# A hybrid decoder layer on one core: the loads of late operands move to ScalarE's DMA queue, and plain output copies enter ScalarE's written order

## The chip, the cores and the metric

The kernel runs on one core of a Trainium2 chip. Its engines work side by side and meet through semaphores: TensorE (PE; its weight loads are PEld), VectorE (DVE), ScalarE (ACT), GpSimd (POOL) and SyncE (SP). Transfers are started by an instruction in the order of one engine (here SP, POOL and, rarely, ACT), and are carried by 16 DMA engines. The metric is the device time of one execution in microseconds (us): the median of the runs shown, 2655.42 us before the change.

## The reference

One layer over 512 tokens of width 2048, in float32. It adds three branches to the residual x, one after the other:

```python
[u | v_sgu | q | k | v_att | g_a | g_b] = rmsnorm(x, attn_norm_g) @ w_in
y_a = u * (tril(W_s) v_norm + b)              # gMLP, chunks of 128
y_b = stick_breaking_attention(q, k, v_att)
x = x + (sigmoid(g_a) * (y_a @ w_up_a) + sigmoid(g_b) * (y_b @ w_up_b)) @ w_o
gate, up = split(rmsnorm(x, ffn_norm_g) @ w_ffn_in)        # hidden width 5632
x = x + (silu(gate) * up) @ w_ffn_out
x = x + sigmoid(rmsnorm(x, ple_norm_g) @ w_ple_gate) * (p @ w_ple)
```

## The kernel before

**Arithmetic.** Activations stand transposed (features on 128 partitions, 512 tokens along a row). Each float32 product is made of three fp32r products of a high and a low part. So every weight block and every operand block is split in two: ACT copies the high part (L369 for weights `whi`, L289 for operands `parts`), and DVE subtracts it to give the low part (L366 `wlo`, L290 `parts`). L385 and L540 are DVE sums of blocks that the cheaper scheme below needs.

**Pairs.** The unit of work is a pair: two 128-wide output tiles, accumulated over units of 256 features. A unit of kind "P" is plain (PE lines L299, L300, L301, three products for each piece). A unit of kind "S" uses a Strassen-like scheme with seven or so products of sums of blocks (PE line L716), whose results are put together from PSUM banks by ACT copies (L739, L772) and DVE adds (L742, L775). A pair may have both kinds: its first part runs plain while the operands' sums are not there yet. `Pair.out()` (L808) finishes a pair. For an all-plain pair it copies two banks with ACT (L814). For a mixed pair `rest()` (L817) adds the two plain banks to the result with DVE (L821).

**Operands.** A form (a set of operand parts of one unit) is built from a block that `load` (L529) fetches from DRAM: `y_form` from the stored y, `spilled_form` (L1392) from the stored mix, x1, hid and x2. A "late" form first makes its plain parts, and later fetches the blocks of sums that were stored beside hid (`second_blocks`, L1379: one transfer of 768 columns and one of 256). `wholes` is the name of every loaded block in the profile.

**Stages**, in us of the profiled execution: the embedding's first pair and start (0 to 92), the w_in pairs with the spatial gating and attention (to 762), the merge with w_up (to 1007), w_o (to 1160), FFN-in (44 pairs, to 2031), FFN-out in three passes over the hidden width, each with its own operands (2031 to 2192, to 2353, to 2490), and the gate (to 2651). At each change of stage PE goes from one set of operands to the next, and that set is loaded and split while PE runs the last pair of the stage behind it.

**Order.** Instructions are traced in the order of the code; a scheduler with a cost model then fixes the order on each engine. `in_turn` binds an ACT or DVE instruction to the one traced before it on that engine, so that such instructions keep the written order. Splits, sums and the copies of the products are in turn; L814 and L821 are not, and the scheduler places them. DMAs go in the order of their issuing engine: SP carries nearly all weights, spills and loads, POOL the accumulating loads (L373), and ACT only the two halves of pT (the layer's input embedding p) at the start. Each DMA that SP or ACT starts is given one of eight completion semaphores in rotation; one that takes a semaphore over waits in its engine's order until that semaphore's last transfer has landed.

Of the kernel before, what the change touches and what calls it, by code (L numbers as in the profile page):

```python
# [14 lines left out]
AF = mybir.ActivationFunctionType  # L15
# [5 lines left out]
T = 512  # L21
# [49 lines left out]
def hybrid_layer(  # L71
# [18 lines left out]
    nc = tc.nc  # L90
# [25 lines left out]
    class Arena:  # L116
# [5 lines left out]
        def take(self, n, how="low"):  # L122


            spots = []
            for start, size in self.holes:
                end = start + size
                if how == "place":
                    start = -(-start // (2 * PLACE)) * 2 * PLACE
                if end - start >= n:  # L130
                    if how == "high":
                        spots.append((-end, end - n))
                    elif how != "old":
                        spots.append((start, start))
                    else:
                        spots.extend((self.given[a // P : -(-(a + n) // P)].max(), a)
                                     for a in {*range(start, end - n + 1, 256), end - n})
            at = min(spots)[1]
            start, size = next(h for h in self.holes if h[0] <= at < h[0] + h[1])
            self.holes.remove((start, size))  # L140
            self.holes.extend(
                h for h in ((start, at - start), (at + n, start + size - at - n)) if h[1])
            return Block(self, at, n)
# [34 lines left out]
    def wide():  # L178
        return tmp.tile([P, 1024], F32, tag="out", name=nm("out"))
# [20 lines left out]
    def mark(instruction):  # L200
        newest[instruction.ins.engine] = instruction.ins.name
# [116 lines left out]
    def in_turn(*instructions):  # L318

        for i in instructions:  # L320
            e = i.ins.engine
            if e in chain:
                tc.add_manual_dep(
                    i.ins, chain[e],
                    mybir.DependencyInfo(mybir.DependencyClass.NoSync,
                                         mybir.DependencyReason.DATA),
                    reason="in its place among the weights")
            chain[e] = i.ins.name
            mark(i)
# [122 lines left out]
    def plain_weights(src):  # L452
        return Weights(src.rearrange("p (b c) -> p b c", b=4), 1, "P")
# [72 lines left out]
    def cut(x):  # L526
        return x.rearrange("p (b c) -> p b c", c=256)

    def load(src, n=1024, how="old"):  # L529
        b = take(n, how)  # L530
        nc.sync.dma_start(out=b.f(0, 1024), in_=src)
        return b

    def gained(dst, src, gi, k):
        return [nc.scalar.activation(dst[:, i * T : (i + 1) * T], src[:, i * T : (i + 1) * T],
                                     AF.Copy, scale=gcol[:, gi + 2 * k + i : gi + 2 * k + i + 1])
                for i in range(2)]
# [97 lines left out]
    def plain_form(src, ready=always, gain=None, raw=1024, how="low", far=False):  # L635
        def steps(form):
            hi, lo = form.blocks = parts.take(1024, how), parts.take(1024, how)
            w = form.raw()
            if gain:
                gained(hi.own(), w.f(), *gain)  # L640
                gi, k = gain
                for i in range(2):
                    a, b = i * T, (i + 1) * T
                    nc.vector.scalar_tensor_tensor(
                        out=lo.own(a, b), in0=w.f(a, b),
                        scalar=gcol[:, gi + 2 * k + i : gi + 2 * k + i + 1], in1=hi.f(a, b),
                        op0=ALU.mult, op1=ALU.subtract)
            else:
                split_into(hi.own(), lo.own(), w.f())
            give(w)  # L650
            return tuple([x.own(0, T), x.own(T)] for x in form.blocks)
            yield

        return Form("P", steps, [(parts, 1024, how)] * 2 + [(wholes, raw, "low")] * bool(raw),
                    ready, src, far)

    class Pair:
# [150 lines left out]
        def out(self, o=None):  # L808
            if self.n["S"]:
                assert o is None  # L810
                return self.rest(self.o)
            o = wide() if o is None else o
            for i, ps in enumerate(self.ends()):
                nc.scalar.activation(o[:, i * T : (i + 1) * T], ps, AF.Copy)  # L814
            return o

        def rest(self, o):  # L817
# [67 lines left out]
    ple_spill = {}  # L885
    ps_p = []

    def ple_raw(queue):
        raw = take(1024, "old")
        for k in (0, T):  # L890
            queue.dma_start(out=raw.f(k, k + T), in_=pT[:, k : k + T])
        return raw

    def ple_operands(raw=None):
        first = raw is not None
        raw = raw or ple_raw(nc.sync)
        ps_p.extend(parts.take(1024, "high") for _ in range(2))
        for k in (0, T):
            ops = split_into(*(x.own(k, k + T) for x in ps_p), raw.f(k, k + T))
            if first:  # L900
                in_turn(*ops)
        give(raw)
# [30 lines left out]
        x_raw.append(take(1024, "old"))  # L933
        nc.sync.dma_start(out=x_raw[-1].f(), in_=xT[len(x_raw) - 1])

    p_raw = ple_raw(nc.scalar)
    nc.scalar.preload_act_table_set("natural_log_exp_and_others")
    ones = consts.tile([P, P], F32, name="ones")
    nc.vector.memset(ones, 1.0)
    warm = small_bank()  # L940
    for _ in range(7):
        nc.tensor.matmul(warm[:, :P], ones, ones, start=True, stop=True)
    w_early = [plain_weights(w_ple[i]) for i in range(3)]
    load_x()
    gcol = consts.tile([P, ng], F32, name="gcol")
    nc.sync.dma_start(out=gcol, in_=gains)
# [99 lines left out]
    y_a, y_b = [None] * 4, [None] * 4  # L1046
    y_spill = [tc.dram_tile([P, 1024], F32, name=nm("y")) for _ in range(4)]
# [283 lines left out]
            plan(w_gate[j], now(GATE, GATE_UNTIL, j))  # L1331

    def y_form(c, i):
        return plain_form((lambda: y_a[i]) if c == "a" else lambda: load(y_spill[i]),
                          lambda: len(y_done) == 8, raw=0 if c == "a" else 1024,
                          far=c == "b")

# [2 lines left out]
    for n, ((w, i), pr) in enumerate(zip(order, made())):  # L1340
# [7 lines left out]
        o = pr.out(block(w, i) if n < 3 else None)  # L1348
# [17 lines left out]
        else:  # L1366
            d = tc.dram_tile([P, 1024], F32, name=nm("gsp"))
# [7 lines left out]
    spill = {(n, j): tc.dram_tile([P, 1024], F32, name=nm(n)) for n in ("mix", "x1", "x2")  # L1375
             for j in range(KU)}
    there, sum_spill = set(), {}

    def second_blocks(d):  # L1379
        blocks = take(768, "old"), take(256, "old")  # L1380
        nc.sync.dma_start(out=blocks[0].f(), in_=d[:, 256:1024])
        nc.sync.dma_start(out=blocks[1].f(), in_=d[:, 0:256])
        return blocks

    def summed_form(kind, n, j):
# [5 lines left out]

    def spilled_form(kind, n, j, gain=None, **how):  # L1392
        return (late_form if kind == "S" else plain_form)(
            lambda size=1024: load(spill[n, j], size), lambda: (n, j) in there, gain, far=True,
            **how)

    def store(n, j, block):
# [79 lines left out]
    for m in range(KH):  # L1477
        if m == KH - 1:
            build(hs[0])
        o = pair(fs, last=m == KH - 1, j=m, until=FFN_UNTIL, doubled=7).out()  # L1480
# [11 lines left out]
    for c, units in enumerate(hs):  # L1492
# [3 lines left out]
        for j in range(KU):  # L1496
# [6 lines left out]
            o = pr.out()  # L1503
            if not end:
                after(2, lambda o=o, j=j: nc.gpsimd.dma_start(
                    out=spill["x1", j], in_=o, accum_op=ALU.add))
# [8 lines left out]
    for j in range(KU):  # L1515
# [36 lines left out]
        else:  # L1552
            o = pair(gs, j=j, until=GATE_UNTIL, doubled=5).out()
# [92 lines left out]
```

## Time and profile before

| | before |
|---|---|
| median of 3 runs | 2655.42 us (2654.60 to 2657.17) |
| profiled execution | 2658.68 us, span 2657.0 us |
| granted TensorE clock, mean | 0.998 |
| PE busy | 2634.6 us, 99% |
| DVE busy | 2265.8 us, 85% |
| ACT busy | 1408.5 us, 53% |
| POOL busy | 455.7 us, 17% |
| DMA moved | 574.32 MB, mean 216 GB/s |

An instruction's row gives its start, its duration, engine, line and tiles, and in brackets the idle time ahead of it with what ended it. Matmuls are pipelined, so the distance between starts, not the duration, is what one costs. A window's row gives its length, the busy time of PE, PEld, DVE, ACT and POOL with the count of instructions, the granted clock, the DMA share and GB/s.

### The profile page before, as it was taken

Reading aid. Unit: us, or ns where it says so; the run is one execution under the profiler, and the core shown is the slowest. Engines: PE = TensorE matmul, PEld = TensorE weight load, DVE = VectorE, ACT = ScalarE, POOL = GpSimd, SP = SyncE. Lnnn points to the kernel's source line nnn. Section 1 sums busy time; section 2 is a strip of 40 time slices with the busy share of each in tenths; the row PEclk is TensorE's granted clock in tenths of the full one; section 3 lists DMA queues with packets and bytes.
Section 4 is the critical chain, followed back from the end, with each engine's and each line's share of the span. In section 5 each row is a group of like instructions: output and inputs, shape, how many; then the busy total and the mean of one; then the engine's idle time right before and its main releaser. Section 6 shows DMA issues by size and latency. Waiting matters only on the chain.

```text
span 2657.0 us, 42520 instructions
## 1 busy us (share of the span) xinstructions
PE 2634.6 (99%) x15197; PEld 2302.2 (87%) x15197; DVE 2265.8 (85%) x3886; ACT 1408.5 (53%) x2263; POOL 455.7 (17%) x565
## 2 busy tenths in 40 slices
PE   9999999999999999999999999999999999999999
PEld 7888888888998888888888888888888888889888
DVE  8687878787887558999999999999999888879798
ACT  7757565655554335465444444444446445455543
POOL 0222323232210001101111111111111211211010
PEclk9999999999999999999999999999999999999999
DMA  6776777777775668987988888888888999988794
GB/s 207 184 195 171 195 171 195 170 191 185 176 190 191 222 222 263 260 245 206 248 223 225 217 219 213 214 220 218 208 224 244 255 227 290 214 249 272 223 269 136
DMA packets 301829, 574.32 MB, mean 216 GB/s; under 512 B 27441, under 2 KB 143921, under 8 KB 301617
## 3 DMA queue, kind: packets, MB, share of 16 engines
q1 hardware_dynamic: 238688, 452.05, 51.8%
q0 software_dynamic: 62640, 119.04, 27.8%
q8 instruction: 119, 1.95, 0.3%
q14 instruction: 94, 0.76, 0.1%
q10 hardware_dynamic: 288, 0.52, 0.1%
HBM read 509.64 MB, written 61.87 MB: 215 GB/s over the span
## 4 chain that ended last, share of the span: by engine, by line
PE 90%; DVE 5%; DMA 2%; ACT 1%; issue 1%; POOL 0%; DVEq 0%; SPq 0%; ACTq 0%; POOLq 0%
PE ps L716 55%; PE ps L301 8%; PE ps L300 8%; PE ps L299 8%; PE small L716 6%; DVE wlo L366 2%; PE small L1196 1%; PE small L1144 1%; DVE out L775 1%; PE small L1070 1%; DVE parts L290 1%; DMA wholes<-hid 1%; DVE wholes L385 1%; DMA wholes<-w_gate 0%; DVE wholes L540 0%
## 5 line engine op out<-in xcount | busy, mean ns | idle before, releaser
L716 PE MATMUL ps<-parts,whi 128*128 128x512 f32 x4486 | 1503.9, 398 | 5.6 <-ACT out L814 3.2
L369 ACT ACTIVATE whi<-wholes 128x512 fp32r<-128x512 f32 (+2 forms) x940 | 873.1, 946 | 742.6 <-DVE wholes L385 300.3
L366 DVE TENSOR_TENSOR wlo<-wholes,whi 128x512 fp32r<-128x512 f32 (+2 forms) x940 | 988.5, 1087 | 91.1 <-ACT whi L369 90.7
L716 PEld LDWEIGHTS ps<-parts,wlo 128*128 128x128 f32 x4486 | 843.1, 188 | 190.9 <-issue 1.9
L716 PE MATMUL ps<-parts,wlo 128*128 128x256 f32 x4486 | 887.9, 279 | 0.6 <-DVE wlo L366 0.6
L716 PEld LDWEIGHTS ps<-parts,whi 128*128 128x128 f32 x4486 | 724.0, 189 | 15.9 <-ACT out L814 3.8
L301 PE MATMUL ps<-parts,wlo 128*128 128x256 f32 (+1 forms) x1546 | 512.8, 333 | 1.1 <-DVE wlo L366 1.1
L300 PE MATMUL ps<-parts,whi 128*128 128x256 f32 (+1 forms) x1546 | 512.8, 332 | 0.7 <-DVE parts L290 0.7
L299 PE MATMUL ps<-parts,whi 128*128 128x256 f32 (+1 forms) x1537 | 509.0, 332 | 3.0 <-ACT parts L289 1.6
L385 DVE TENSOR_TENSOR wholes<-wholes 128x256 f32<-128x256 f32 x832 | 353.0, 424 | 15.5 <-DMA wholes<-w_ffn_out 0.8
L775 DVE TENSOR_TENSOR out<-out,ps 128x256 f32<-128x256 f32 x537 | 222.2, 417 | 131.8 <-ACT out L772 131.3
L300 PEld LDWEIGHTS ps<-parts,whi 128*128 128x128 f32 x1546 | 292.1, 189 | 35.1 <-DVE parts L290 1.7
L299 PEld LDWEIGHTS ps<-parts,whi 128*128 128x128 f32 x1537 | 290.7, 189 | 31.7 <-ACT parts L289 2.3
L301 PEld LDWEIGHTS ps<-parts,wlo 128*128 128x128 f32 x1546 | 292.4, 189 | 28.6 <-DVE wlo L366 1.5
L373 POOL DMA_DIRECT2D wholes<-w_ffn_in x169 | 147.3, 871 | 705.2 <-DVE wholes L385 216.7
L373 POOL DMA_DIRECT2D wholes<-w_in x132 | 117.5, 893 | 543.4 <-DMA wholes<-w_in 165.7
L716 PE MATMUL small<-parts,whi 128*128 128x512 f32 x496 | 197.0, 397 | 0.0
L772 ACT ACTIVATE out<-ps 128x256 f32<-128x256 f32 x285 | 105.8, 383 | 61.1 <-PE ps L716 52.0
L290 DVE TENSOR_TENSOR parts<-wholes,parts 128x1024 fp32r<-128x1024 f32 (+3 forms) x147 | 124.9, 867 | 12.2 <-ACT parts L289 12.1
L289 ACT ACTIVATE parts<-wholes 128x768 fp32r<-128x768 f32 (+3 forms) x147 | 107.9, 764 | 49.1 <-DVE wholes L540 19.2
L373 POOL DMA_DIRECT2D wholes<-w_ffn_out x70 | 61.0, 871 | 348.1 <-DVE out L775 68.6
L1458 ACT ACTIVATE out<-out 128x512 f32<-128x512 f32 x44 | 27.8, 632 | 174.0 <-DVE out L1265 174.0
(136 smaller groups left out, 1843.7 us busy)
## 6 DMA issues: line engine op xcount, KB each, us to landing
wholes<-w_ffn_in SPq DMA_DIRECT2D x169, 384.0 KB, 5.6
wholes<-w_in SPq DMA_DIRECT2D x132, 384.0 KB, 4.9
wholes<-w_ffn_in SPq DMA_DIRECT2D x169, 256.0 KB, 4.6
wholes<-w_ffn_in POOLq DMA_DIRECT2D x169, 256.0 KB, 5.4
wholes<-w_in SPq DMA_DIRECT2D x132, 256.0 KB, 3.9
wholes<-w_in POOLq DMA_DIRECT2D x132, 256.0 KB, 4.9
wholes<-w_ffn_out SPq DMA_DIRECT2D x70, 384.0 KB, 6.4
wholes<-x SPq DMA_DIRECT2D x46, 512.0 KB, 5.9
```

The lines of the kernel that those rows point to most:

```text
L289: return (nc.scalar.activation(hi, src, AF.Copy), nc.vector.tensor_tensor(out=lo, in0=src, in1=hi.bitcast(F32), op=ALU.subtract))
L290: nc.vector.tensor_tensor(out=lo, in0=src, in1=hi.bitcast(F32), op=ALU.subtract))
L299: nc.tensor.matmul(ps, sh, mh, start=start, stop=False)
L300: nc.tensor.matmul(ps, sh, ml, start=False, stop=False)
L301: return nc.tensor.matmul(ps, sl, mh, start=False, stop=stop)
L366: in_turn(nc.vector.tensor_tensor(out=self.lo[:, blocks], in0=r, in1=h.bitcast(F32), op=ALU.subtract))
L369: in_turn(nc.scalar.activation(h, r, AF.Copy))
L373: nc.gpsimd.dma_start(out=raw[:, 3:5], in_=self.src[:, 1:3], accum_op=ALU.add)
L385: in_turn(nc.vector.tensor_tensor(out=o, in0=x, in1=y, op=ALU.add))
L716: m = nc.tensor.matmul(out, l, r, start=first and k == 0, stop=last and k == 1)
L772: in_turn(nc.scalar.activation(out, x, AF.Copy, scale=scale))
L775: in_turn(nc.vector.tensor_tensor(out=out, in0=x, in1=y, op=op))
```

## The change

`load` gets a queue. The blocks of y, mix, x1, hid and x2 for operand forms, and both transfers of `second_blocks`, are started by ACT in place of SP: 112 transfers (4 of y, 16 of mix, 16 of x1, 22 first blocks of hid, 40 for second blocks of hid, 14 of x2). The residual and gate loads stay with SP. The L814 copies, 16 of them, enter ACT's written order. At the start, the second half of pT goes to SP, behind the first weights of the embedding.

```diff
-    def load(src, n=1024, how="old"):
+    def load(src, n=1024, how="old", queue=nc.sync):
         b = take(n, how)
-        nc.sync.dma_start(out=b.f(0, 1024), in_=src)
+        queue.dma_start(out=b.f(0, 1024), in_=src)
...
             for i, ps in enumerate(self.ends()):
-                nc.scalar.activation(o[:, i * T : (i + 1) * T], ps, AF.Copy)
+                in_turn(nc.scalar.activation(o[:, i * T : (i + 1) * T], ps, AF.Copy))
...
-    def ple_raw(queue):
+    def ple_raw(*queues):
         raw = take(1024, "old")
-        for k in (0, T):
-            queue.dma_start(out=raw.f(k, k + T), in_=pT[:, k : k + T])
+        for k, q in zip((0, T), queues):
+            q.dma_start(out=raw.f(k, k + T), in_=pT[:, k : k + T])
...
-    p_raw = ple_raw(nc.scalar)
+    w_early = [plain_weights(w_ple[0])]
+    p_raw = ple_raw(nc.scalar, nc.sync)
...
-    w_early = [plain_weights(w_ple[i]) for i in range(3)]
+    w_early.extend(plain_weights(w_ple[i]) for i in range(1, 3))
...
     def y_form(c, i):
-        return plain_form((lambda: y_a[i]) if c == "a" else lambda: load(y_spill[i]),
+        return plain_form((lambda: y_a[i]) if c == "a" else lambda: load(y_spill[i], queue=nc.scalar),
...
-        nc.sync.dma_start(out=blocks[0].f(), in_=d[:, 256:1024])
-        nc.sync.dma_start(out=blocks[1].f(), in_=d[:, 0:256])
+        nc.scalar.dma_start(out=blocks[0].f(), in_=d[:, 256:1024])
+        nc.scalar.dma_start(out=blocks[1].f(), in_=d[:, 0:256])
...
-            lambda size=1024: load(spill[n, j], size), lambda: (n, j) in there, gain, far=True,
+            lambda size=1024: load(spill[n, j], size, queue=nc.scalar), lambda: (n, j) in there, gain, far=True,
```

The lines behind about L940 count one more after the change (L1460 is L1461 and so on). The order of instructions shifts on every engine, also where no edited line stands. Three places follow; `wlo` and `whi` are parts of weights, `parts` those of operands, `ps` and `small` PSUM banks, `out` a pair's result.

DVE, early in FFN-in, just behind its first pair; before:

```order
L366 TENSOR_TENSOR wlo1_78<-wholes_74,whi1_77 128x512
L1460 TENSOR_TENSOR out_1275_11137<-out_1275_11137 128x512
L290 TENSOR_TENSOR parts_73<-wholes_74,parts_73 128x3x256
L385 TENSOR_TENSOR wholes_74<-wholes_74 128x256
L540 TENSOR_TENSOR wholes_74<-wholes_74 128x256
L385 TENSOR_TENSOR wholes_74<-wholes_74 128x256
L540 TENSOR_TENSOR wholes_74<-wholes_74 128x256 x2
L290 TENSOR_TENSOR parts_73<-wholes_74,parts_73 128x256
L540 TENSOR_TENSOR wholes_74<-wholes_74 128x256
L366 TENSOR_TENSOR wlo0_76<-wholes_74,whi0_75 128x1280
```

And after the change:

```order
L366 TENSOR_TENSOR wlo1_78<-wholes_74,whi1_77 128x512
L1461 TENSOR_TENSOR out_1275_11137<-out_1275_11137 128x512
L385 TENSOR_TENSOR wholes_74<-wholes_74 128x256
L821 TENSOR_TENSOR out_1277_11141<-ps_1287_11189,out_1277_11141 128x512
L385 TENSOR_TENSOR wholes_74<-wholes_74 128x256
L540 TENSOR_TENSOR wholes_74<-wholes_74 128x256
L290 TENSOR_TENSOR parts_73<-wholes_74,parts_73 128x3x256
L540 TENSOR_TENSOR wholes_74<-wholes_74 128x256 x2
L366 TENSOR_TENSOR wlo0_76<-wholes_74,whi0_75 128x1280
```

The L821 of bank ps_1287 stood some twenty rows further down, behind the split of `wlo2`, and now stands between two sums, ahead of the split of `wlo0`.

ACT, at the change from the first pass of FFN-out to the second; before:

```order
L369 ACTIVATE whi0_75<-wholes_74 128x512
L289 ACTIVATE parts_73<-wholes_74 128x3x256
L289 ACTIVATE parts_73<-wholes_74 128x256
L289 ACTIVATE parts_73<-wholes_74 128x3x256
L289 ACTIVATE parts_73<-wholes_74 128x256
L814 ACTIVATE out_1939_20536<-ps_1894_20364 128x512
L369 ACTIVATE whi2_79<-wholes_74 128x1280
L369 ACTIVATE whi2_79<-wholes_74 128x512
L814 ACTIVATE out_1939_20536<-ps_1895_20365 128x512
```

And after the change:

```order
L1382 DMA wholes_74<-hid_1199_10947 128x768
L1383 DMA wholes_74<-hid_1199_10947 128x256
L289 ACTIVATE parts_73<-wholes_74 128x3x256
L289 ACTIVATE parts_73<-wholes_74 128x256
L1382 DMA wholes_74<-hid_1200_10948 128x768
L1383 DMA wholes_74<-hid_1200_10948 128x256
L289 ACTIVATE parts_73<-wholes_74 128x3x256
L289 ACTIVATE parts_73<-wholes_74 128x256
L814 ACTIVATE out_1939_20536<-ps_1894_20364 128x512
L814 ACTIVATE out_1939_20536<-ps_1895_20365 128x512
L369 ACTIVATE whi2_79<-wholes_74 128x1280
```

The two L814 copies now follow each other, ahead of both pieces of `whi2`; the loads of second blocks stand in ACT's order between the splits.

DVE, in the gate's second pair; before:

```order
L1531 TENSOR_TENSOR out_2217_23176<-out_2217_23176,wholes_74 128x1024
L1537 TENSOR_TENSOR out_2217_23176<-out_2217_23176,wholes_74 128x1024 x2
L385 TENSOR_TENSOR wholes_74<-wholes_74 128x256 x2
L366 TENSOR_TENSOR wlo1_78<-wholes_74,whi1_77 128x1280
L366 TENSOR_TENSOR wlo1_78<-wholes_74,whi1_77 128x512
```

And after the change:

```order
L1532 TENSOR_TENSOR out_2217_23176<-out_2217_23176,wholes_74 128x1024
L821 TENSOR_TENSOR out_2220_23182<-ps_2231_23232,out_2220_23182 128x512
L1538 TENSOR_TENSOR out_2217_23176<-out_2217_23176,wholes_74 128x1024
L821 TENSOR_TENSOR out_2220_23182<-small_2236_23248,out_2220_23182 128x512
L1538 TENSOR_TENSOR out_2217_23176<-out_2217_23176,wholes_74 128x1024
L385 TENSOR_TENSOR wholes_74<-wholes_74 128x256 x2
L366 TENSOR_TENSOR wlo1_78<-wholes_74,whi1_77 128x1280
```

Before, the two L821 came after the splits of `wlo1` and `wlo0` and three L290; now they stand between the closing steps of the first pair (L1532, L1538), ahead of the sums and the split of `wlo1`.

More of the change, by code (lines that the diff above doesn't have):

```diff
@@ L895, in ple_operands @@
         first = raw is not None
-        raw = raw or ple_raw(nc.sync)
+        raw = raw or ple_raw(nc.sync, nc.sync)
         ps_p.extend(parts.take(1024, "high") for _ in range(2))
```

## The prediction, made before the changed kernel was run

> **What bounds the kernel now.** I read the page first, then PE's table of waits, then the timelines of the places named there.
>
> ```profile
> span 2657.0 us, 42520 instructions
> PE 2634.6 (99%) x15197; PEld 2302.2 (87%) x15197; DVE 2265.8 (85%) x3886; ACT 1408.5 (53%) x2263; POOL 455.7 (17%) x565
> ...
> PE 90%; DVE 5%; DMA 2%; ACT 1%; issue 1%; POOL 0%; DVEq 0%; SPq 0%; ACTq 0%; POOLq 0%
> ```
>
> PE is busy 2634.6 of 2657.0 us, so it bounds, and all idle time of PE together is 22.4 us. The change adds or removes no matmul, hence it can win only a part of these 22.4 us, while a new stall of PE has no such ceiling.
>
> ```profile
> PE ps L716 <- ACT out L814: 3.2, 2, 2.0
> PE small L1255 <- ACT wholes L1093: 2.8, 1, 2.8
> PE ps L716 <- DVE out L821: 1.6, 2, 0.8
> PE ps L299 <- DVE out L821: 1.4, 1, 1.4
> ...
> PE ps L301 <- DVE wlo L366: 1.1, 1, 1.1
> ...
> PE small L716 <- DVE wlo L366: 0.7, 1, 0.7
> ```
>
> The columns are total, times and longest. What the change touches is the first row (L814 becomes ordered) and the L821 rows (nothing of L821 is edited, but the schedule around it moves). Together 6.2 us.
>
> **What the queue itself is worth.** The loads change their issuing engine, not their bytes.
>
> ```profile
> wholes<-w_ffn_out SPq DMA_DIRECT2D x70, 256.0 KB, 5.5
> wholes<-w_ffn_out POOLq DMA_DIRECT2D x70, 256.0 KB, 5.7
> wholes<-hid SPq DMA_DIRECT2D x22, 512.0 KB, 7.6
> ```
>
> A 256 KB load of the same tensor lands 5.5 us after issue from SP and 5.7 us from POOL, so another queue buys no transfer time here; I take the same 7.6 us for a hid block from ACT. The Trainium skill, page "DMA: Bandwidth & Descriptors", section "Issuing engines are not separate DMA queues", speaks against the change in the same sense: transfers run on the same 16 engines whoever starts them, and several issuers save only issue time. By that rule alone the sum would be 0, and this pair of rows agrees with it. What the change moves is therefore the place in an order: a load on ACT can go ahead of SP's weights, but waits for whatever ACT instruction stands before it. I go through the stages.
>
> **Start: -1.2 us (bounds -1.2 and 0).**
>
> ```profile
> 23.84 0.50 PE L301 MATMUL ps<-parts,wlo 128*128 128x512 f32 x1 [1.07 <-DVE wlo L366]
> ```
>
> PE waits 1.07 us for a `wlo` of the embedding. In the new order this split stands ahead of two small DVE instructions of the norm, and its `whi` likewise on ACT, so it is ready before PE asks: the stall goes, with a little re-use. If the pT half on SP lands later, nothing is won. In the merge the four y loads cost between -0.5 and +0.5, nearest to 0.
>
> **w_o: +0.7 us (-1.6 to +1.2).**
>
> ```profile
> 1048.23 2.09 DVE L366 TENSOR_TENSOR wlo<-wholes,whi 128x1280 fp32r<-128x1280 f32 x2
> ```
>
> PE's two 0.8 us waits for L821 lie around this row. Now both L821 come after a 2.09 us split, while PE has about 18 matmuls of the next weights first. On ACT a load of mix or x1 waits for the store of x1 to land, and a product's copy (L739) stands behind it. By my chain the stall is about 2.3 in place of 1.6; +1.2 if ACT is held longer, -1.6 if not at all.
>
> **FFN-in: +2.3 us (-0.3 to +2.5).**
>
> ```profile
> 1206.17 0.42 DVE L385 TENSOR_TENSOR wholes<-wholes 128x256 f32<-128x256 f32 x1
> ...
> 1207.53 0.39 PE L301 MATMUL ps<-parts,wlo 128*128 128x512 f32 x1
> ...
> 1206.00:1226.00 20.00, 19.89 (x110) 16.90 (x108) 20.00 (x39) 11.95 (x18) 2.60 (x3) 1.00 0.67 181
> ```
>
> The L821 of bank ps_1287 now stands directly behind the L385 that ends about 1205.6 (without the L290 of 1205.31 ahead of it). The bank's last product starts 1207.53 and ends 1207.92. So DVE stands still for 2.3 us, in a stretch of 20 us where it is busy 20.00 us, and at whose end PE already waits 0.7 us for a `wlo` (the last row of the waits). Nothing hides it: +2.3, or -0.3 if L821 no longer delays the wait it heads now.
>
> **FFN-out's first pass: +2.0 us (0 to +6).**
>
> ```profile
> 2037.30 1.06 ACT L369 ACTIVATE whi<-wholes 128x1024 fp32r<-128x1024 f32 x1 [2.96 <-PE ps L300]
> 2053.66 0.58 ACT L814 ACTIVATE out<-ps 128x512 f32<-128x512 f32 x1
> ...
> 2020.00:2030.00 10.00, 10.00 (x58) 8.70 (x57) 9.18 (x13) 6.65 (x10) 0.40 (x1) 1.00 0.80 261
> ```
>
> Two loads that SP started some ten us earlier now stand in ACT's order behind the L369 of 2037.30, which waits 2.96 us for PE. The splits of their blocks now precede L814, which I expect at about 2062 in place of 2053.66 (ten us less about two of slack). Against that, the new order gives PE 24 matmuls of the next pair ahead of the product that needs the bank.
>
> ```profile
> 2213.00 0.39 PE L716 MATMUL ps<-parts,wlo 128*128 128x256 f32 x2
> ...
> 2213.69 0.40 PE L716 MATMUL ps<-parts,wlo 128*128 128x256 f32 x2
> ...
> 2214.62 0.40 PE L716 MATMUL ps<-parts,whi 128*128 128x512 f32 x1
> 2216.98 0.50 PE L716 MATMUL ps<-parts,whi 128*128 128x512 f32 x1 [1.96 <-ACT out L814]
> 2219.14 0.80 PE L716 MATMUL ps<-parts,whi 128*128 128x512 f32 x1 [1.20 <-ACT out L814]
> ```
>
> Four such matmuls take 0.69 us (2213.00 to 2213.69), 24 take 4.2. The product came at about 2056.4 and without a stall, and now comes at 2060.6; L814 ends at 2062.6: +2.0. If the loads wait for one landing less it is 0; if they meet one more (7.6 us), less 2 us of slack, about +6.
>
> **Second pass: -3.9 us (-6.1 to 0).** Here stand both L814 waits, in the rows above: 1.96 and 1.20, together 3.2 us. On ACT:
>
> ```profile
> 2215.06 1.38 ACT L289 ACTIVATE parts<-wholes 128x768 fp32r<-128x768 f32 x2 [1.38 <-DMA wholes<-hid]
> 2216.35 0.58 ACT L814 ACTIVATE out<-ps 128x512 f32<-128x512 f32 x1
> 2216.82 1.78 ACT L369 ACTIVATE whi<-wholes 128x1280 fp32r<-128x1280 f32 x2
> 2218.50 0.58 ACT L814 ACTIVATE out<-ps 128x512 f32<-128x512 f32 x1
> ```
>
> The second copy waits for 1.78 us of weight splits, which now come behind it; and PE's need moves from 2214.85 by 4.2 us to 2219.0. But the copies also stand behind one more pair of loads and splits; by my chain they end near 2221, a stall of about 2.2 us in place of 3.2: -1.0. To this belongs the clock:
>
> ```profile
> 2216.00:2220.00 4.00, 1.82 (x7) 1.37 (x8) 3.21 (x5) 3.98 (x7) 0.09 (x1) 0.80 1.07 337
> 2220.00:2224.00 4.00, 4.00 (x14) 3.42 (x14) 3.67 (x8) 2.85 (x5) 1.69 (x2) 0.50 1.06 356
> ...
> 640.00:644.00 4.00, 4.00 (x27) 3.60 (x27) 2.46 (x6) 3.25 (x8) 0.93 (x1) 1.00 0.76 119
> ```
>
> After the two waits the granted clock is 0.50, and PE does 14 matmuls in 4 us where 21 and more are usual; I price this stretch at 2.9 us (4 us at 0.50, some at 0.80 on both sides, less the idle part). After the 2.8 us wait at L1255 the clock stayed 1.00. So a stall of 2.2 us should not trigger it, and -2.9 is added: -3.9. It is -6.1 when the stall goes whole, and 0 when it stays. The third pass, whose second blocks come two to three us later: +0.5 (-0.3 to +1.5).
>
> **Gate: +5.7 us (-0.5 to +6.6).**
>
> ```profile
> 2517.79 1.22 DVE L1531 TENSOR_TENSOR out<-out,wholes 128x1024 f32<-128x1024 f32 x1
> 2521.48 2.48 DVE L1537 TENSOR_TENSOR out<-out,wholes 128x1024 f32<-128x1024 f32 x2 [2.47 <-ACT out L1534]
> 2523.88 0.88 DVE L385 TENSOR_TENSOR wholes<-wholes 128x256 f32<-128x256 f32 x2
> 2524.67 2.09 DVE L366 TENSOR_TENSOR wlo<-wholes,whi 128x1280 fp32r<-128x1280 f32 x2
> ...
> 2530.82 0.69 DVE L821 TENSOR_TENSOR out<-ps,out 128x512 f32<-128x512 f32 x1
> ...
> 2524.98 0.39 PE L301 MATMUL ps<-parts,wlo 128*128 128x512 f32 x1
> ...
> 2526.79 0.40 PE L716 MATMUL ps<-parts,wlo 128*128 128x256 f32 x2
> ```
>
> DVE now meets the L821 of ps_2231 behind L1531 (ended 2519.0) and waits there until PE closes that bank (2524.98 + 0.39 = 2525.4). Then follow L821 0.69, L1537 1.24, L821 0.69, L1537 1.24, L385 0.88 and the first piece of `wlo`, 1.4 of the 2.09: 2531.5. PE needs it at 2526.79, so it waits 4.7 us, where before it waited 1.4 for L821 a little later: +3.3. The following pair's split, behind a sigmoid and the same chain, comes by the same steps about 0.6 later than its need: +3.9. A stall of 4.7 us is longer than the 3.2 that ended in half clock above, so I add a part of the 2.9, 1.8. The Trainium skill, page "TensorE: Matmul & The Clock Gate", section "Part 1: The HAM clock gate", tells that the clock falls after a whole idle window of about 3.4 us; this profile shows a fall after two waits of 1.96 and 1.20 with work between them, so the row does not fit a single idle window, and by the page's rule the term would be 2.9 or 0.
>
> **The sum.** -1.2 + 0 + 0.7 + 2.3 + 2.0 - 3.9 + 0.5 + 5.7 = +6.1 us, against the profiled execution (2658.68 us, span 2657.0 and 1.7 around it): 2664.8. That execution lies 3.3 us over the median of 2655.42, so the median should be about **2661.5**.
>
> **Rivals.**
> - *No transfer earlier, nothing later* (same engines, 5.5 against 5.7): the 24 matmuls cover the first pass (2.0 gone), FFN-in finds slack (2.3 gone), the gate's stall doesn't bring the clock down (1.8 gone). 6.1 - 6.1 = 0: 2655.4. For it speaks that PE hides most things today; against it that DVE is at 20.00 of 20 us in FFN-in.
> - *PE's lead decides, on the faster side.* With L814 done before PE's later need, the second pass wins 3.2 + 2.9 = 6.1, w_o 1.6, the start 1.2; FFN-in costs 1.0 and the gate 2.0 where DVE's other work fills its wait. -5.9: 2649.5. It decides from the point where both copies end by 2219.0.
> - *ACT held by landings.* Its loads wait for semaphores of SP's transfers at each change of pass: first pass +6, second 0, w_o +1.2, third +1.5, the rest as forecast: 6.1 + 4 + 3.9 + 0.5 + 1 = +15.5, some 2 of it beside other stalls: about 2669.
>
> **How the numbers follow.** Forecast 0.45, nothing 0.25, faster rival 0.18, held ACT 0.12. A difference of 0.2%, 5.3 us, is about what a measurement of this kernel can tell from none. The forecast (2656 to 2667 by its bounds) lies to a third under that mark: 0.15 same, 0.30 slower. So faster 0.18, same 0.15 + 0.25 = 0.40, slower 0.30 + 0.12 = 0.42. The range takes in the faster rival's point and most of held ACT: 2649 to 2668.
>
> **What would show it.** In the waits after: L814's row falls from 3.2 to about 2, and the clock stays 1.00 around 2220; `wlo` L366 becomes PE's largest wait, with some 4.7 us near 2527 and 2 us near 1230; DVE waits for PE ahead of L821 at both. L814 of the first pass lies near 2062. If `wlo` shows no such wait, the gate's term is wrong and the sum falls to about zero; if L814 waits vanish as well, the faster rival holds.

## The result, and the profile after

The changed kernel is slower: 2680.23 us median of 6 runs (2675.45 to 2683.4) against 2656.79 of 6 runs before (2654.6 to 2659.62), ratio **1.0086 (95% interval 1.0073 to 1.0099)**, 23.4 us. The forecast was 2661.5 in a range of 2649 to 2668: the sign was right, the size a quarter of what came. The profiled execution took 2678.9 us, 20.2 more than that of before.

The page of the changed kernel, its lines on span, busy time and chain:

```profile
span 2677.2 us, 42518 instructions
PE 2644.5 (99%) x15197; PEld 2303.9 (86%) x15197; DVE 2267.7 (85%) x3886; ACT 1408.2 (53%) x2263; POOL 452.3 (17%) x565
...
PE 87%; DMA 5%; DVE 5%; ACT 1%; issue 1%; POOL 0%; ACTq 0%; DVEq 0%; SPq 0%; POOLq 0%
```

The same 15197 matmuls; PE's idle time rose from 22.4 to 32.7 us, and its busy time by 9.9 us, though the work is the same. Some 3 us of the 9.9 are the clock: apart from the start and the end, TensorE ran 13.7 us at half clock (2214.2 to 2217.6, 2541.8 to 2548.7, 2579.4 to 2582.8) where before it ran 6.8 us (2218.4 to 2225.2), and each such us does half the work. The rest lies in spacings of matmuls at full clock that are too small for the table of waits; its cause is open. DMA's share of the chain rose from 2% to 5%. PE's largest waits after the change, and two that shrank (total, times, longest):

```profile
PE ps L716 <- ACT whi L369: 4.0, 2, 3.5
PE ps L716 <- DVE wlo L366: 3.7, 3, 2.2
PE ps L299 <- ACT parts L289: 3.6, 3, 2.1
PE ps L716 <- DVE out L821: 3.0, 1, 3.0
...
PE small L1256 <- ACT wholes L1094: 0.5, 1, 0.5
PE ps L716 <- ACT out L814: 0.3, 1, 0.3
```

L814's 3.2 us are gone, as the ordered copies were to do. Four other rows of 3 to 4 us stand in its place. Since both profiles hold the same number of matmuls, the start of the n-th in one can be set against the n-th in the other; how much this delay grew in each stage:

| stage (us, before) | forecast | profile |
|---|---|---|
| start, to 92 | -1.2 | +1.5 |
| w_in, to 640 | not in the sum | -2.0 |
| merge, to 1007 | 0 | +0.2 |
| w_o, to 1200 | +0.7 | +2.7 |
| FFN-in's start, to 1300 | +2.3 | +2.4 |
| FFN-in's rest, to 2031 | 0 | +0.6 |
| first pass, to 2192 | +2.0 | +2.9 |
| second pass, to 2353 | -3.9 | +0.5 |
| third pass, to 2490 | +0.5 | +3.5 |
| gate | +5.7 | +7.8 |
| sum | +6.1 | +20.2 |

One profile of each is compared here, and single runs of one kernel lie up to 11 us apart; the -2.0 of w_in is such a thing (PE's wait at L1255, 2.8 us before and 0.5 now, lies between none and 2.8 us in runs that don't touch it). The parts are therefore priced by medians below.

**The hid loads.** The load of the first hid block, as SP started it in the timeline of before:

```profile
1227.74 0.38 SPq L531 DMA_DIRECT2D wholes<-hid  x1
```

After the change:

```profile
2023.69 0.33 ACTq L531 DMA_DIRECT2D wholes<-hid  x1
```

This block lay ready for 800 us; now its load is started some ten us before the pass needs it. At the second pass ACT and then PE stand still among such loads (timeline of the changed kernel; in brackets the idle time and what ended it):

```profile
2204.11 0.33 ACTq L531 DMA_DIRECT2D wholes<-hid  x1
...
2211.03 0.33 ACTq L1383 DMA_DIRECT2D wholes<-hid  x1
2211.40 1.06 ACT L289 ACTIVATE parts<-wholes 128x1024 fp32r<-128x1024 f32 x1 [5.28 <-DMA wholes<-w_ffn_out]
...
2212.51 0.73 PE L299 MATMUL ps<-parts,whi 128*128 128x512 f32 x2 [2.10 <-ACT parts L289]
```

ACT stood still for 5.28 us ahead of the split at 2211.40; the load L1383, which comes before it in ACT's order, could not be started until 2211.03, and the bracket names a landing of weights, of which SP and POOL start the loads, as what ended the wait. So this stall is ACT held by a landing, beside the lateness of the first blocks; the experiments below try the lateness without ACT. PE's 2.10 and, just around it, 0.38 and 0.53 us for the operands' low parts are together about as long as the two L814 waits that went.

**w_o.** ACT, DVE and PE of the changed kernel around 1050:

```profile
1037.11 0.33 ACTq L531 DMA_DIRECT2D wholes<-mix  x1
1037.48 1.09 ACT L739 ACTIVATE out<-ps 128x512 f32<-128x512 f32 x2 [5.90 <-DMA x<-wholes]
...
1038.11 0.42 DVE L742 TENSOR_TENSOR out<-out 128x256 f32<-128x256 f32 x1 [5.54 <-ACT out L739]
...
1051.95 2.08 DVE L366 TENSOR_TENSOR wlo<-wholes,whi 128x1280 fp32r<-128x1280 f32 x2
1053.96 1.28 DVE L821 TENSOR_TENSOR out<-ps,out 128x512 f32<-128x512 f32 x2
...
1054.79 0.47 PE L716 MATMUL ps<-parts,whi 128*128 128x512 f32 x1 [3.02 <-DVE out L821]
```

A load of mix waits on ACT until a store of x1 has landed, and the product's copy L739 behind it stands 5.90 us. DVE waits 5.54 us for that copy and is busy from there on without a break, so both L821, behind the 2.08 us split, come late, and PE stands 3.02 us in place of 1.6.

**Gate.** DVE, PE and the windows (us, busy time of five engines, clock, DMA share, GB/s) of the changed kernel:

```profile
2531.69 1.22 DVE L1532 TENSOR_TENSOR out<-out,wholes 128x1024 f32<-128x1024 f32 x1
2537.39 0.69 DVE L821 TENSOR_TENSOR out<-ps,out 128x512 f32<-128x512 f32 x1 [4.49 <-PE ps L301]
...
2541.66 2.08 DVE L366 TENSOR_TENSOR wlo<-wholes,whi 128x1280 fp32r<-128x1280 f32 x2
...
2542.46 0.80 PE L716 MATMUL ps<-parts,whi 128*128 128x512 f32 x1 [3.52 <-ACT whi L369]
...
2540.00:2544.00 4.00, 1.54 (x4) 1.09 (x5) 3.93 (x6) 2.22 (x4) 0.00 (x0) 0.73 0.92 306
2544.00:2548.00 4.00, 4.00 (x13) 3.39 (x13) 4.00 (x9) 2.59 (x5) 0.00 (x0) 0.50 0.75 213
```

DVE stands 4.49 us ahead of L821 until PE closes the bank. The sums of the next weights follow behind it, then ACT's high part of these sums (`whi`, L369), for which PE waits 3.52 us; then PE runs at half clock.

### The profile page after: what moved, and what is told of

Its sections match the earlier page's. It is cut to its first block, busy times and chain, and to the rows that moved or that the text cites. A ratio compares the mean times of both kernels' runs of the same rounds, so it can differ in the third digit from the quotient of the medians.

```text
span 2677.2 us, 42518 instructions
## 1 busy us (share of the span) xinstructions
PE 2644.5 (99%) x15197; PEld 2303.9 (86%) x15197; DVE 2267.7 (85%) x3886; ACT 1408.2 (53%) x2263; POOL 452.3 (17%) x565
## 4 chain that ended last, share of the span: by engine, by line
PE 87%; DMA 5%; DVE 5%; ACT 1%; issue 1%; POOL 0%; ACTq 0%; DVEq 0%; SPq 0%; POOLq 0%
PE ps L716 54%; PE ps L300 8%; PE ps L301 8%; PE ps L299 8%; PE small L716 6%; DMA wholes<-hid 2%; DVE wlo L366 2%; PE small L1145 1%; DVE parts L290 1%; PE small L1197 1%; PE small L1071 1%; DVE wholes L385 1%; DMA wholes<-w_gate 1%; DVE out L775 1%; ACT whi L369 0%
## 5 line engine op out<-in xcount | busy, mean ns | idle before, releaser
L369 ACT ACTIVATE whi<-wholes 128x512 fp32r<-128x512 f32 (+2 forms) x940 | 873.1, 946 | 752.8 <-DVE wholes L385 299.4
L290 DVE TENSOR_TENSOR parts<-wholes,parts 128x256 fp32r<-128x256 f32 (+3 forms) x147 | 123.3, 862 | 29.6 <-ACT parts L289 29.4
L289 ACT ACTIVATE parts<-wholes 128x768 fp32r<-128x768 f32 (+3 forms) x147 | 108.6, 765 | 66.8 <-DMA wholes<-hid 22.7
```

What stands on the lines that cost most here:

```text
L289: return (nc.scalar.activation(hi, src, AF.Copy), nc.vector.tensor_tensor(out=lo, in0=src, in1=hi.bitcast(F32), op=ALU.subtract))
L290: nc.vector.tensor_tensor(out=lo, in0=src, in1=hi.bitcast(F32), op=ALU.subtract))
L369: in_turn(nc.scalar.activation(h, r, AF.Copy))
```

## The experiments

The theory after the result: the loads lose their early place. In the kernel before, `tick()` binds what is traced in it on an engine with ordered instructions (PE, ACT, DVE) behind the last of them; SP has none, so there the scheduler could put a load wherever its data and its block of memory allowed:

```python
            if i.engine in units:
                tc.add_manual_dep(i, units[i.engine], ...)
```

Rivals: ACT's queue itself is the cost; the adds L821, which the schedule now places early; any change of the schedule costs. All runs, each against the kernel before on the same chip (medians, us):

| run | median | before | ratio, 95% interval |
|---|---|---|---|
| copies_in_order | 2656.88 | 2657.13 | 0.9999 (0.9990 to 1.0008) |
| embedding_split | 2657.47 | 2657.13 | 1.0001 (0.9992 to 1.0010) |
| loads_on_act | 2676.42 | 2657.13 | 1.0064 (1.0052 to 1.0077) |
| after_adds_in_order | 2680.17 | 2657.13 | 1.0082 (1.0068 to 1.0096) |
| hid_first_blocks | 2665.47 | 2656.22 | 1.0034 (1.0022 to 1.0047) |
| hid_second_blocks | 2655.53 | 2656.22 | 0.9997 (0.9988 to 1.0006) |
| x1_loads | 2662.17 | 2656.22 | 1.0019 (1.0010 to 1.0028) |
| x2_loads | 2660.95 | 2656.22 | 1.0016 (1.0007 to 1.0025) |
| after_loads_unbound | 2678.53 | 2656.14 | 1.0083 (1.0070 to 1.0095) |
| hid_late_on_sp | 2666.45 | 2656.14 | 1.0039 (1.0026 to 1.0051) |
| x2_loads_adds_in_order | 2658.48 | 2656.14 | 1.0009 (1.0000 to 1.0018) |
| second_blocks_and_copies | 2657.58 | 2656.14 | 1.0005 (0.9996 to 1.0013) |
| hid_first_unbound | 2659.15 | 2657.40 | 1.0005 (0.9997 to 1.0014) |
| x1_unbound | 2661.86 | 2657.40 | 1.0017 (1.0009 to 1.0026) |
| after_three_kinds_back | 2663.01 | 2657.40 | 1.0022 (1.0014 to 1.0031) |
| before_adds_in_order | 2656.70 | 2657.40 | 0.9998 (0.9989 to 1.0006) |
| x1_unbound_adds_in_order | 2660.73 | 2656.97 | 1.0013 (1.0004 to 1.0022) |
| mix_and_y_loads | 2662.60 | 2656.97 | 1.0022 (1.0013 to 1.0030) |

### The three parts of the change, one at a time

Each is the edit of the change with the other two left out.

> The kernel before, with only the L814 copies bound to ACT's written order; all loads stay with SP. Theory one (the moved loads make the loss): within 3 us of before, the second pass of FFN-out may win 1 to 3 us because the second copy no longer stands behind 1.78 us of weight splits. Theory two (any change of the schedule costs, the queue is not needed for it): +5 us or more.

> The kernel before, with only the second half of pT on SP behind the first weights of the embedding. Both theories: the first 30 us as in the changed kernel, where PE stood still for 1.75 us at 25.9 waiting for whi, in place of 1.07 us at 23.8 for wlo, so about +1 us there. Theory one: +1 to +2 us in all. Theory two (any change of the schedule costs): +5 us or more, since DVE's and ACT's orders shift through all later stages too.

> The kernel before, with only the 112 loads moved to ACT's queue; copies unordered, pT as before. Theory one: nearly the whole loss, +17 to +22 us (ratio 1.007 to 1.008): w_o +2.7, FFN-in +2.6, FFN-out's first pass +3, its third +3, gate +5 to +8. Theory two: less than half of it, under +10 us.

The copies cost -0.3 us, the split +0.3, the loads +19.3 (these intervals reach 2 to 3.5 us to either side, and so do those below). So the loads are the loss, and a changed schedule alone is not: the split moved DVE's and ACT's order through all later stages and the time stayed.

### Which loads

`load` gets the queue for one tensor only, or only `second_blocks` is edited:

```diff
-            lambda size=1024: load(spill[n, j], size), lambda: (n, j) in there, gain, far=True,
+            lambda size=1024: load(spill[n, j], size, queue=nc.scalar if n in ('hid',) else nc.sync), lambda: (n, j) in there, gain, far=True,
```

> The kernel before, with only the 22 first blocks of hid loaded on ACT's queue. Before, SP fetched 6 of the first pass's 600 to 800 us ahead of their use and 11 of the other passes' 130 us ahead; on ACT all stand within some 20 us of the change of pass. Theory one (prefetch lost): most of FFN-out's loss, +5 to +8 us, with waits of PE for L289 and L290 at 2070, 2210 and 2380. Theory two (ACT is held by the second blocks' loads, which pass between its splits): within 3 us of before.

> The kernel before, with only the 40 loads of second blocks of hid on ACT's queue; the first blocks stay with SP. Theory one (prefetch lost): within 3 us of before, since SP fetched these at the change of pass already. Theory two (ACT is held by them): most of FFN-out's loss, +5 to +8 us, and L814's waits longer than the 3.2 us of before.

> The kernel before, with only the 16 loads of x1 operands on ACT. They come up to 40 us later in the changed kernel, and DVE stood still there for some 3 us more between 1160 and 1200, waiting for ACT's L554 and L739, ahead of a stretch where it is busy throughout. Expected: +2.5 us at FFN-in's start and +2 us in w_o, +4 to +5 us in all; DVE's early L821 at 1205 costs none of it, because DVE comes to it later. The other theory, that the early L821 makes FFN-in's loss: DVE stands 2 us still ahead of that L821.

> The kernel before, with only the 14 loads of x2 operands on ACT. The L821 of the gate stand early again here, ahead of the split of wlo1, as in the changed kernel. If that place makes the gate's loss: +4 to +6 us, all of it between 2520 and 2580, with a wait of PE for whi or wlo of 3 us or more. If the gate's loss comes from FFN-out's delays and not from this place: within 2 us of before.

> The kernel before, with only the loads of mix and y on ACT. They are the part left over of after_three_kinds_back (+5.6 us) that was not tried alone. If the loss there is theirs: +3 to +6 us, with a wait of PE for L821 of 2 to 3 us in w_o near 1052. If it comes only with the split of pT and the ordered copies beside them: within 2 us of before.

First blocks of hid +9.3, x1 +6.0, x2 +4.7, mix with y +5.6, second blocks -0.7. With copies and split the parts sum to 25.0, near the 23.4 of the whole; the loads by themselves sum to 24.9 against the 19.3 of loads_on_act, a difference that five such intervals don't tell from none. The second blocks, whose loads pass between ACT's splits and which I had taken for the trouble, cost nothing while the first blocks stay with SP. PE's waits in hid_first_blocks between 2031 and 2500, the whole of FFN-out, are these:

```profile
PE ps L716 <- ACT out L814: 6.5, 2, 4.3
PE ps L300 <- DVE parts L290: 2.3, 2, 1.9
```

Before, L814's 3.2 us were all but 0.2 of PE's waits there. The time came out as expected, the waits only in part: the late splits hold up the copies L814 on ACT (2.2 us at 2058, 4.3 at 2222), where waits for L289 and L290 were expected; only the one near 2380 is of that kind. In x2_loads PE waits 2.26 us for `whi` at 2525, a little less than the 3 us expected. In x1_loads w_o did not grow by the n-th matmul, against the +2 us expected there.

For mix the mechanism of w_o shows again, in the timeline of mix_and_y_loads (ACT, then PE):

```profile
1035.21 1.09 ACT L739 ACTIVATE out<-ps 128x512 f32<-128x512 f32 x2 [6.49 <-DMA x<-wholes]
...
1052.64 0.47 PE L716 MATMUL ps<-parts,whi 128*128 128x512 f32 x1 [2.91 <-DVE out L821]
```

The changed kernel with hid's first blocks, x1 and x2 back on SP agrees with it:

> The changed kernel with the loads of hid's first blocks, x1 and x2 back on SP; second blocks, mix, y, the ordered copies and the split of pT as in the changed kernel. If the three kinds are the whole loss (9.3 + 6.0 + 4.7): within 3 us of before. If the parts cost more together than alone: +4 us or more.

It came to +5.6 us, the second of the answers expected. But mix and y, which that expectation had left out, cost 5.6 us by themselves, so no extra cost of the parts together is needed.

### Place or queue

hid late on SP, and hid early on ACT:

```diff
+        if late:    # n == 'hid'; the load stays on nc.sync
+            tc.add_manual_dep(d.ins, asked[-1], ...)
```

```diff
-            if i.engine in units:
+            if i.engine in units and i.name not in free:    # free: names of the loads
```

> The kernel before, with the loads of hid still on SP, each bound behind the last weight load asked for when it was traced, so that none is fetched 600 us ahead. If losing the prefetch makes the loss: +6 to +10 us with no load on ACT at all. If ACT's queue makes it: within 3 us of before.

> As hid_first_blocks (+9.3 us: only the 22 first blocks of hid on ACT), but these loads are exempt from the rule that binds them behind ACT's last ordered instruction; in ACT's order the first pass's stand some 500 rows earlier. If their place makes the loss: within 3 us of before. If a load of hid on ACT costs by its queue, early or late: +6 us or more.

These two part the theories. SP without the early place costs +10.3 us; ACT's queue with the early place costs +1.8, not told from zero (by its interval at most 3.7). The first hid load in the timeline of hid_late_on_sp:

```profile
2018.68 0.43 SPq L531 DMA_DIRECT2D wholes<-hid  x1
```

And in that of hid_first_unbound:

```profile
1226.06 0.34 ACTq L531 DMA_DIRECT2D wholes<-hid  x1
```

PE's waits follow the place as well. Between 2031 and 2500, hid_late_on_sp (whose lines count six more, so that L820 is L814):

```profile
PE ps L722 <- ACT out L820: 6.2, 3, 4.3
PE ps L300 <- DVE parts L290: 1.8, 3, 0.7
PE ps L722 <- DVE parts L290: 1.3, 1, 1.3
PE ps L722 <- ACT parts L289: 1.2, 1, 1.2
```

And hid_first_unbound:

```profile
PE ps L716 <- ACT out L814: 3.3, 2, 2.1
PE ps L716 <- DVE parts L290: 1.2, 1, 1.2
PE ps L300 <- DVE parts L290: 0.8, 1, 0.8
```

For hid's first blocks it is the place, not the queue. The same for all loads of the changed kernel at once:

> The changed kernel, with the loads of y, mix, x1, hid and x2 exempt from the rule by which tick binds everything that it traces on ACT behind ACT's last ordered instruction; they stay on ACT's queue. In its order the first pass's loads of hid then stand some 500 rows earlier again. If the binding (the place in ACT's order) makes the loss, and not the queue: the 9 us of hid's first blocks and the 5 of x1 go, +2 to +6 us over before stay (the gate's early L821 is still there). If ACT's queue itself makes the loss: +20 us as the changed kernel.

It stayed at +22.4, against the expected +2 to +6. That expectation counted on most of x1's cost going with hid's. By the runs with one tensor alone, x1 keeps 4.5 us without the binding (below) and hid 1.8; if x2 and mix with y keep their 4.7 and 5.6, 16.6 us were to be expected, and some 6 us come on top. In its profile the first pass's operands come in time, but PE has new waits, for the products' sums (its table of waits):

```profile
PE ps L716 <- DVE out L775: 5.3, 5, 2.0
PE ps L716 <- ACT whi L369: 4.0, 2, 3.5
PE ps L716 <- DVE out L821: 3.7, 2, 3.2
PE ps L716 <- DVE p L775: 3.6, 3, 1.4
```

and ACT, in the timeline, waits for weights just ahead of one of them, where five hid loads had been started on ACT from 2081.8 to 2088.2:

```profile
2105.52 1.27 ACT L369 ACTIVATE whi<-wholes 128x1280 fp32r<-128x1280 f32 x1 [5.06 <-DMA wholes<-w_ffn_out]
```

That the loads on ACT push aside SP's weights there is my reading of these rows; it wasn't tried by itself. So lifting the binding is no remedy for the whole.

### x1, x2 and the early adds

> As x1_loads (+6 us: only the x1 loads on ACT), unbound in the same way; the early L821 at FFN-in's start stays where it was in x1_loads. If the late x1 loads make the loss: within 2 us of before. If the early L821 makes it: +4 to +6 us.

> As x1_unbound (+4.5 us), and the L821 adds bound to DVE's written order, so that at FFN-in's start they stand behind the split of wlo0. If x1's loss is the late loads and the early L821 together: within 2 us of before. If any load of x1 on ACT costs DVE its waits for ACT there: +4 us again.

Each came out at the second of its two answers: +4.5 and +3.8 us remain of 6.0, so neither the late loads nor the early L821 is shown to be most of x1's cost. What stays is work that DVE loses ahead of the stretch where it is busy throughout. The window 1150 to 1200 in five kernels (the third busy time, behind PE's and PEld's, is DVE's); before:

```profile
1150.00:1200.00 50.00, 50.00 (x268) 43.07 (x267) 46.80 (x80) 38.03 (x55) 4.68 (x5) 1.00 0.82 260
```

The changed kernel:

```profile
1150.00:1200.00 50.00, 49.84 (x269) 42.79 (x268) 43.94 (x75) 33.24 (x49) 3.82 (x4) 1.00 0.74 236
```

The run x1_loads:

```profile
1150.00:1200.00 50.00, 49.84 (x261) 42.52 (x260) 43.58 (x77) 35.71 (x52) 5.28 (x6) 1.00 0.80 252
```

The run x1_unbound:

```profile
1150.00:1200.00 50.00, 50.00 (x263) 42.69 (x262) 44.83 (x79) 36.85 (x53) 4.69 (x5) 1.00 0.77 236
```

The run x1_unbound_adds_in_order:

```profile
1150.00:1200.00 50.00, 50.00 (x266) 42.75 (x265) 44.84 (x78) 35.80 (x52) 4.69 (x5) 1.00 0.77 238
```

DVE does 46.80 us of work there before, 43.6 to 44.8 with x1 on ACT; in the runs that move only hid's first blocks, x2, or mix with y it does 46.7 to 46.8. The 2 to 3 us are missing when PE asks for splits near 1230: by the n-th matmul, the stretch from 1200 to 1300 grew by 2.9 us in x1_loads, 2.2 in x1_unbound and 1.9 in x1_unbound_adds_in_order, and by at most 0.4 in those three others. So this is about half of what x1 costs; where the rest falls is open. DVE's waits between 1150 and 1200 in x1_loads:

```profile
DVE out L742 <- ACT out L739: 2.3, 1, 2.3
DVE parts L555 <- ACT parts L554: 2.0, 1, 2.0
```

Before, these two are 1.3 and 0.5 us. In x1_unbound they are 1.4 and 0.7, and two others have come in their place:

```profile
DVE mean L1012 <- PE small L1008: 1.4, 1, 1.4
DVE wholes L540 <- ACT wholes L535: 1.1, 1, 1.1
```

So lifting the binding moved the waits and did not end them. What makes the new ones is open.

> The kernel before with the x2 loads on ACT, as in the run x2_loads (+4.7 us), and the L821 adds bound to DVE's written order, which puts those of the gate behind the split of wlo1 again. If their early place makes the loss: within 2 us of before, no wait of PE for whi L369 near 2525. If the x2 loads on ACT make it: +4 to +5 us again.

> The kernel before with only the L821 adds bound to DVE's written order. In the changed kernel this took the gate's wait away and yet won nothing in all. If the bound adds cost elsewhere as much as they won there: +3 to +6 us. If they cost nothing by themselves: within 2 us of before, and the missing gain stays open.

> The changed kernel with the L821 adds bound to DVE's written order: in the gate they stand behind the split of wlo1 again, early in FFN-in behind wlo0, while all loads stay on ACT. If the early place of L821 makes the losses of w_o, FFN-in and gate, these go: 8 to 11 us faster than the changed kernel, about +12 us over before, no 3.5 us wait of PE near 2542. If the loads' place in ACT's order makes them, as the changed kernel: +20 to +23 us.

With x2 on ACT, ordering the adds takes +4.7 to +2.3: about half, though the two intervals overlap, and against the expectation a wait for `whi` of 1.9 us stays in place of 2.3. Ordering them costs nothing before (-0.7). In the changed kernel it shortened the gate's wait for `whi` from 3.52 to 1.94 us, yet the median didn't move (+23.0). Its profile, of the slowest of its five runs, shows the gate growing by 2.3 us in place of 7.8, but w_o, all of FFN-in and the first pass together by 16.9 in place of 8.6. One profile of each doesn't tell whether the ordered adds make that loss, so where the gain went stays open.

### A version under both

> The kernel before with the two parts that cost nothing alone: second blocks of hid on ACT and the L814 copies in order. By both theories between -3 and +1 us; it is the candidate for a version under before.

+1.4 us, not told from before. No version tried is shown to be faster than before.

## Why the prediction was right or wrong

**What bounds, and the ceiling.** Right: PE bounds; the L814 row fell from 3.2 to 0.3, while new stalls had no such ceiling. The "2656 to 2667 by its bounds" does not follow from the terms: their bounds, added end to end, give 2645 to 2674. The measured 2680 lies above both.

**What the queue is worth.** Right for hid: the place in an order, not the queue, moves the time (hid_late_on_sp, hid_first_unbound). For x1 it is not shown: x1_unbound keeps 4.5 us. The Trainium skill, page "DMA: Bandwidth & Descriptors", section "Issuing engines are not separate DMA queues", says that transfers run on the same 16 DMA engines whichever engine starts them; hid_first_unbound's +1.8 us, not told from zero, agrees with it.

**The passes: the step that failed.** The prediction counted two loads that come ten us later at the first pass, and gave the second pass -3.9. It put the other first blocks of hid at nothing, without a reason: in the profile of before 6 of them are loaded 600 to 800 us ahead of the first pass and 10 some 130 us ahead of the later passes (the expectation of hid_first_blocks says 11), and all of these came to the change of pass. The passes were forecast at -1.4 together and came to +6.9 in the profile; by medians the first blocks alone cost 9.3, the largest part of what the forecast missed.

What the prediction did reckon with at the passes came near. The first pass's L814 started at 2066.4, about 2061 on the scale of before, where 2062 was forecast; PE waited 0.3 us for it, and 1.09 us at 2078 for a split (L289) behind the landing of a hid block. At the second pass L814's waits went, but PE now waits earlier, for the operands themselves, and half clock came all the same (0.77 and 0.80 in the two windows of 4 us from 2212). With the first blocks back on SP and the second blocks on ACT, the second pass of the profile is 3.9 us (hid_second_blocks) and 4.4 us (after_three_kinds_back) shorter than before and stays at 1.00: there the forecast -3.9 holds. These are single profiles, and in hid_second_blocks' median (-0.7) no gain is told from none.

**w_o.** Mechanism right (a load on ACT behind the x1 store's landing, L739 behind it, both L821 after a split), size too small: 3.02 us of wait where 2.3 was forecast. In mix_and_y_loads it cost 5.6 us where +0.7 was forecast, part of it half clock, for which the term had nothing.

**FFN-in.** The size was right (+2.4 for +2.3), the step wrong: DVE did not wait ahead of the early L821, because it came there late. It had lost 2.9 us of work between 1150 and 1200, and x1_unbound_adds_in_order, with L821 behind the split, kept 3.8 of x1's 6.0 us.

**Gate.** Right step by step up to the wait: DVE stood 4.49 us ahead of L821, and the clock fell to 0.50. PE's wait was 3.52 us (4.7 forecast), and it was for the high part `whi`, which ACT makes from the same late sums, and not for `wlo`. A wait of 2.2 us for `wlo` at the third pair (2578) was larger than the 0.6 allowed: +7.8 in place of +5.7. In the medians x2 alone cost 4.7 us, of which about half went with the ordered adds.

**Start.** Wrong: PE waited 1.75 us for whi at 25.9 where a stall of 1.07 was to vanish. In the median it is worth nothing (embedding_split, +0.3).

**Rivals.** "ACT held by landings" (2669, chance 0.12) was nearest in number. Its mechanism shows in the rows (5.90 us of idle ACT in w_o, 5.28 at the second pass), but it isn't hid's main loss: hid_late_on_sp costs 10.3 us with no load on ACT. Its price for the second pass (0) was about right, those for w_o (+1.2) and the third pass (+1.5) were too small. A range that took it in whole would still have missed by 11 us.

## What to carry to other kernels

Before a load moves to another engine's queue, look at how far ahead of its use it stands in the old order and where it will stand in the new: a queue whose engine does nothing else can fetch early, as SP did here, and a scheduler that keeps a written order on the new engine may take that away (9 to 10 us of 2657 here, on either queue). An engine that computes and also starts loads is held by the landings its loads must await, and so are the engines that wait for it (5.90 us of idle time on ACT became 3.02 on PE). Where an order is printed for many rows, go through all moved loads and price each kind, not the two nearest to a known stall.

## What the runs showed of the hardware

The same length of wait was followed by half clock in one run and not in another. After PE's wait of 3.02 us that ends at 1054.79 the changed kernel kept 1.00; after 2.91 us that end at 1052.64 the run mix_and_y_loads fell. What differs is where the wait lies. The granted clock in the profiles of this case changes only on a grid with steps of 3.41 us, and the grid lies differently in each execution. The windows of the changed kernel, cut at its steps:

```profile
1050.23:1053.64 3.41, 1.54 (x10) 1.09 (x8) 3.41 (x7) 1.28 (x4) 1.67 (x2) 1.00 0.84 203
1053.64:1057.06 3.41, 2.27 (x13) 2.06 (x14) 3.41 (x7) 0.54 (x1) 0.06 (x1) 1.00 1.05 262
```

And of mix_and_y_loads, at its own:

```profile
1050.39:1053.80 3.41, 1.16 (x7) 1.08 (x8) 3.41 (x6) 0.44 (x2) 0.18 (x1) 1.00 0.95 315
1053.80:1057.21 3.41, 3.41 (x13) 2.94 (x12) 3.04 (x5) 2.58 (x3) 1.33 (x2) 0.50 0.95 278
```

In the changed kernel the wait falls into two steps of the grid, with 1.87 us idle in the first and 1.14 in the second; in mix_and_y_loads 2.25 us fall into one, and the next step runs at 0.50. Over the 20 profiles of this case, all 29 steps at full clock in which PE's waits add up to 1.88 us or more were followed by half clock, and 5 of the 69 with 1.00 to 1.87 us; apart from the start and the end of an execution no other step was. It also fits the rows of the prediction: the 2.8 us before L1255 lie as 1.2 and 1.5 us in two steps and the clock stayed, and the waits of 1.96 and 1.20 us put 2.4 us into one and it fell. So how long PE waits within one step decides in nearly all cases, and neither the kernel nor the length of a single wait does. A step at 0.50 does the work of 1.7 us: by the n-th matmul, w_o grew by 2.7 us in the changed kernel and by 4.5 in mix_and_y_loads.
